# Zero-padded operands on TensorE in a two-layer diffusion backbone on one core

## The chip, the core and the metric

The kernel runs on one core of one Trainium2 chip. The core has a matrix engine (TensorE, PE in the profile, with its weight loads shown apart as PEld), three engines for elementwise work (VectorE is DVE, ScalarE is ACT, GpSimd is POOL) and a queue processor for transfers (SyncE is SP). The metric is the device time of one execution in microseconds (us); lower is better. A difference under 0.3% (8 us here) can't be told from no change for this kernel.

## The reference

One inference step of a backbone with two layers and a width of 2048, for 512 latent tokens and 128 prompt tokens (640 columns in all). Each layer normalizes its input, multiplies it by one input projection of 7168 columns, gives the result to three groups of heads, and multiplies their outputs by one output projection.

```python
h = rmsnorm(x, norm_g) * (1 + scale) + shift
proj = jnp.matmul(h, w_in)                      # 2048 x 7168
q, k, v, ag, lx, lg, hv, hx1, hx0, hg = jnp.split(proj, SPLITS, axis=-1)
# differential attention: 8 heads, two components of 64 features each
s = jnp.einsum('bqhcd,bkhcd->bchqk', qblk, k) * scale
p = jax.nn.softmax(s, axis=-1)
w = p[:, 0] - lam * p[:, 1]
att = jnp.einsum('bhqk,bkhe->bqhe', w, v)
# hyena: a filter network gives two long filters, used through a spectrum
filt = jnp.matmul(hdn, w3).reshape(L, 2, HY_W) * decay      # hdn has 64 features
y = irfft(rfft(u, n=2 * L) * rfft(g, n=2 * L), n=2 * L)[:, :L]
...
return x + gate * jnp.matmul(concat([att, lru, hy]), w_out)
```

A latent query of the attention sees 256 cached keys and 512 latent keys (768); a prompt query sees the 128 prompt keys.

## The kernel before

Features lie on the 128 partitions and tokens on the columns. All matrix products are made at float32 accuracy from operands in two parts, `hi` (rounded to the engine's reduced float32) and `lo` (the rest): a product is hi x hi + hi x lo + lo x hi, three matmuls into the same accumulator (`mm3`, L715; `mms`, L707).

**The main product.** `gemm` (L401) makes 128 output features of a projection: 4 pieces of 4 chunks of the contraction; for each chunk 6 matmuls of 320 columns (L419, tile `g`). The weights of a piece come by a DMA (`wr`), ACT rounds them (`wh`, L177) and DVE makes the rest (`wl`, L178); there are four buffers of each. Between the pieces stand steps of `ada_steps` (L321), which computes the modulation of later phases on DVE (`adas`, L334).

**Attention.** `attention` (L1034) runs for 8 heads in each layer: projections of the queries, keys and values, rotation of queries and keys (`rope_rot`, L1023, on DVE, with scratch tiles `rs` and `rt`), the split of the queries of each component c into `qq` (64 rows of hi above 64 rows of lo, for c = 1 the other way round), and of the keys into `kk` (hi twice, on all 128 rows) and `kl` (lo, one tile, each component on its own 64 rows). `softmax_diff` (L1140) works on a block of 128 queries: for each component, two halves of 384 keys, and for each half two matmuls into PSUM tile `pS`: `kk` on 128 rows (hi x hi and lo x hi at once), and `kl` on 64 rows (`qq[c][cs]`, `kl[cs]`). These four are called a score group here; the prompt's has one half of 128 keys, so two matmuls. DVE then takes the row maximum out of `pS` (L1157), ACT the exponential with its sum `Z` (L1158), DVE the two normalizations and the difference (L1161 to L1164); the weights are turned by six transposes (L1100), split (`wth`, `wtl`) and multiplied by the values (18 matmuls). There is one buffer of `pS`. A head ends with the squares of its output: a product on POOL into `oq` (L1119), a square on ACT and a difference on POOL (L1121).

**Hyena.** `filters` (L571) makes the spectra of the filters: `filt` multiplies the 64 rows of the hidden layer `hid` by `w3` (L607; positions 0 to 383 on the lower partitions, the others on the upper ones), and `spec` multiplies by the tables of a Fourier transform (`tb`); time 256 stands apart, as products with a single row (`eh` and `el` against one row of the table `rw`). `hyena_u` (L752) makes the signal, with `ue` for time 256 (two rows); `hyena_conv` (L802) makes its spectrum (products with `ue`, two rows), multiplies, and transforms back (products with `rh` and `rl`, one row each). The frequency 512 is a product with one column of weights, into one row of PSUM. `filter_hidden` (L544) computes `hid` of both layers at the start and keeps it on chip.

The order on each engine is set by a scheduler from the program's text and its priorities; an engine takes its instructions in that order. The steps of the hyena filters and of the long convolution stand between the pieces of `gemm` calls.

## Time and profile before

| what | value |
|---|---|
| time, median of 3 runs | 2831.08 us (2827.84 to 2836.65) |
| profiled execution, span from first to last instruction | 2832.2 us |
| granted TensorE clock, mean | 0.988 of full speed |
| PE busy | 2722.8 us, 96% of the span |
| PEld busy | 2496.4 us, 88% |
| DVE busy | 1937.1 us, 68% |
| ACT busy | 1074.7 us, 38% |
| POOL busy | 246.7 us, 9% |

The span is the profiled execution's own time as far as the profile has it; it lies 1.1 us above the median. A matmul's record reaches from its start to its end, and the next one starts long before that, since they are pipelined: what a matmul costs PE is the distance from its start to the next start, not its duration. A row of the timeline merges equal instructions that follow each other ("x4"), and shows the start of the first and the time to the end of the last. "64*128" is the part of the array that a matmul uses, rows by columns. The number of columns behind it ("64x384") is what it streams.

### The profile page before, as it was taken

The numbers are of one execution on the slowest core, as the hardware profiler recorded it, in microseconds if no ns is written. First come the engines' busy times: TensorE is split into PE (matmuls) and PEld (weight loads), VectorE is DVE, ScalarE is ACT, GpSimd is POOL, SyncE is SP. The second block draws the span as 40 slices with busy tenths as digits, with TensorE's granted clock in tenths as the row PEclk, the third lists the DMA queues.
The fourth block names the chain that finished last, engine by engine and source line by source line (L and its number), as shares of the span: only waits on it lengthen the run. The fifth ranks groups of instructions, "written<-read, shape, count | busy, mean of one in ns | idle before, by whom it ended". The sixth has DMA issues, their size and how long they took to land. (4 is left out here: it accounts for less than half of the span.)

```text
span 2832.2 us, 45809 instructions
## 1 busy us (share of the span) xinstructions
PE 2722.8 (96%) x17539; PEld 2496.4 (88%) x17539; DVE 1937.1 (68%) x3507; ACT 1074.7 (38%) x1970; POOL 246.7 (9%) x332
## 2 busy tenths in 40 slices
PE   5999989999999999999999999999999999999998
PEld 3689888889888888899988999888888899889998
DVE  3578996876877787787779467867776655555333
ACT  4234544444444212132234255444444432213223
POOL 1001210000000220200001022000000021020000
PEclk9999999999999999999999999999999999999999
DMA  8863442322323544476665323322222142335333
GB/s 257 269 211 113 119 147 64 95 81 70 95 79 100 165 131 144 151 239 204 194 182 156 94 81 92 112 73 90 80 66 59 56 147 77 96 122 175 95 90 122
DMA packets 439271, 353.54 MB, mean 125 GB/s; under 512 B 26710, under 2 KB 367326, under 8 KB 438796
## 3 DMA queue, kind: packets, MB, share of 16 engines
q1 hardware_dynamic: 428618, 336.39, 39.2%
q10 hardware_dynamic: 9298, 9.03, 1.0%
q0 software_dynamic: 1136, 5.19, 0.5%
q8 instruction: 138, 2.26, 0.3%
q14 instruction: 81, 0.66, 0.1%
HBM read 315.60 MB, written 34.93 MB: 124 GB/s over the span
## 5 line engine op out<-in xcount | busy, mean ns | idle before, releaser
L419 PE MATMUL g<-A,wh 128*128 128x320 f32 x8320 | 1622.8, 313 | 0.7 <-DVE A L178 0.7
L419 PEld LDWEIGHTS g<-A,wh 128*128 128x128 f32 x8320 | 1316.0, 189 | 24.8 <-issue 18.0
L419 PE MATMUL g<-A,wl 128*128 128x320 f32 x4160 | 968.1, 312 | 0.0
L177 ACT CAST wh<-wr 128x512 fp32r<-128x512 f32 (+1 forms) x592 | 361.9, 613 | 1049.3 <-PE g L419 802.4
L419 PEld LDWEIGHTS g<-A,wl 128*128 128x128 f32 x4160 | 700.8, 189 | 9.3 <-issue 7.8
L178 DVE TENSOR_TENSOR wl<-wr,wh 128x512 fp32r<-128x512 f32 (+1 forms) x592 | 435.2, 738 | 389.9 <-ACT wh L177 369.1
L334 DVE SCALAR_TENSOR_TENSOR adas<-wa,cs,adas 128x512 f32<-128x512 f32 x480 | 360.2, 777 | 56.5 <-DMA wa<-in_w_ada 55.0
L1158 ACT ACTIVATE e<-e,mx 128x768 f32<-128x768 f32 (+1 forms) x160 | 133.5, 834 | 71.7 <-DVE e L1157 71.0
L1157 DVE TENSOR_SCALAR_CACHE_REDUCE e<-pS 128x768 f32<-128x768 f32 (+1 forms) x160 | 131.3, 821 | 38.7 <-PE pS L709 37.0
L709 PE MATMUL pS<-kl,qq 64*128 64x384 f32 (+1 forms) x288 | 122.6, 426 | 0.0
L709 PE MATMUL pS<-kk,qq 128*128 128x384 f32 (+1 forms) x288 | 109.0, 379 | 2.9 <-DVE e L1157 2.7
L1119 POOL TENSOR_TENSOR oq<-ot 128x640 f32<-128x640 f32 x16 | 22.2, 1389 | 1007.8 <-ACT ot L1115 559.8
L520 PE MATMUL gp<-A,wh 128*128 128x320 f32 x512 | 101.4, 316 | 1.0 <-ACT wh L177 1.0
L396 PE MATMUL g<-A,wh 128*128 128x320 f32 (+2 forms) x384 | 92.8, 324 | 8.2 <-DVE A L491 5.7
L709 PEld LDWEIGHTS pS<-kl,qq 64*128 64x128 f32 x288 | 52.7, 183 | 54.3 <-issue 50.9
L178 DVE TENSOR_TENSOR wtl<-pt,wth 128x512 fp32r<-128x512 f32 (+1 forms) x144 | 70.5, 524 | 42.6 <-ACT wth L177 42.2
L520 PEld LDWEIGHTS gp<-A,wh 128*128 128x128 f32 x512 | 79.2, 188 | 22.5 <-issue 10.6
L177 ACT CAST wth<-pt 128x512 fp32r<-128x512 f32 (+1 forms) x144 | 59.8, 459 | 87.1 <-PE pt L1100 84.9
L709 PEld LDWEIGHTS pS<-kk,qq 128*128 128x128 f32 x288 | 54.1, 188 | 29.0 <-issue 23.7
L396 PEld LDWEIGHTS g<-A,wh 128*128 128x128 f32 x384 | 67.1, 194 | 13.6 <-DVE A L491 7.9
L1389 DVE SCALAR_TENSOR_TENSOR xf<-g,mod,xo 128x128 f32<-128x128 f32 (+3 forms) x96 | 38.4, 434 | 56.5 <-PE g L419 23.9
L312 PE MATMUL pa<-wada,csw 128*32 128x512 f32 (+1 forms) x320 | 51.6, 562 | 23.7 <-DMA wada<-in_w_ada 23.5
(353 smaller groups left out, 3187.6 us busy)
## 6 DMA issues: line engine op xcount, KB each, us to landing
wr<-in_w_in SPq DMA_DIRECT2D x440, 256.0 KB
wa<-in_w_ada SPq DMA_DIRECT2D x256, 256.0 KB
wada<-in_w_ada SPq DMA_DIRECT2D x64, 512.0 KB
wr<-in_w_out SPq DMA_DIRECT2D x128, 256.0 KB
mx<-md SPq DMA_DIRECT2D x28, 320.0 KB
md<-ot SPq DMA_DIRECT2D x16, 320.0 KB
gm<-md SPq DMA_DIRECT2D x16, 320.0 KB
R<-rd SPq DMA_DIRECT2D x16, 320.0 KB
```

The lines of the kernel that those rows point to most:

```text
L177: self.nc.scalar.copy(hi, src)
L178: self.nc.vector.tensor_tensor(lo, src, hi.bitcast(F32), op=ALU.subtract)
L312: nc.tensor.matmul(acc[32 * q:32 * q + 32, :], lhsT=self.csw[:, k, :], rhs=w[:, j, :], start=k < 4, stop=k >= 12, tile_position=(0, 32 * q))
L334: nc.vector.scalar_tensor_tensor(acc[:, s], w, c, acc[:, s], op0=ALU.mult, op1=ALU.add)
L396: nc.tensor.matmul(p[:, j, o:o + c1 - c0], lhsT=w[:, c, :], rhs=rhs[k][x][:, c0:c1], start=(a == 0 and c == 0 and n == 0), stop=(a == 3 an ...
L419: nc.tensor.matmul(p[:, j, :HT], lhsT=w[:, c, :], rhs=rhs[k][x][:, j * HT:(j + 1) * HT], start=(a == 0 and c == 0 and n == 0), stop=(a == ...
L520: nc.tensor.matmul(p[:, j, :HT], lhsT=w[:, c, :], rhs=rhs[k0 + c][x][:, j * HT:(j + 1) * HT], start=(c == 0 and t == 0), stop=(c == n - 1 ...
L709: self.nc.tensor.matmul(out, lhsT=a, rhs=b, start=(n == 0), stop=(n == len(pairs) - 1))
L1119: nc.gpsimd.tensor_tensor(sq, ot, ot, op=ALU.mult)
L1157: V.tensor_scalar(e[:, :nk].rearrange("p (a b) -> p a b", a=nhf), ps[:, :nhf, :hw], -1.0, None, op0=ALU.mult, op1=ALU.min, accum_out=mx)
L1158: nc.scalar.activation(e[:, :nk], e[:, :nk], AF.Exp, scale=-1.0, bias=mx, accum_out=Z[:, c:c + 1])
L1389: V.scalar_tensor_tensor(x[:, a:b], p, mod[:, 32 + m, s:s + 1], xo[:, a:b], op0=ALU.mult, op1=ALU.add)
```

## The change

The operands that used 64, 32 or fewer rows of the array, or one column, are put into tiles of 128 partitions whose other rows are zero, and the products run over all 128 rows and 128 columns.

- Scores: `kl` becomes two tiles, one for each component, allocated once in a layer; the 64 rows that belong to the other component are set to zero once (POOL, 64 x 896 each). To make room, the scratch tile `rt` of `rope_rot` goes away and its values go to the buffer of `oq`.
- Filter network: `w3` gets two copies, each with the other 64 rows zero, and the product runs over all of `hid`. `hid` is written to DRAM at the start, and read back when `filters` begins.
- Spectra of the filters: `eh` and `el` become rows 0 and 32 of one tile `er`; the table row in `rw` stands on partitions 0 and 32 of a 128-partition table that is zero elsewhere. Two matmuls become one.
- The long convolution: `ue` has its parts on rows 0 and 32, made after the transposition and no longer before it; `rh` and `rl` become rows 0 and 32 of `rr`, and again two matmuls become one.
- Frequency 512: 128 columns of weights in the place of one; only row 0 of the result is read.

```diff
-    rowt = np.zeros((2, TCE_W + 256), f4)
-    rowt[:, 0:257] = tab(np.cos, np.array([256]), fe, 512)
...
+    rowt = np.zeros((128, TCE_W + 256), f4)
+    for p0 in (0, 32):
+        rowt[p0, 0:257] = tab(np.cos, np.array([256]), fe, 512)[0]
...
-            hid = self.tl(self.cst, [128, 384], s="hid") if b else self.tl(pool, [128, 384], tag="h1", bufs=2)
+            hid = self.tl(pool, [128, 384], tag="h1", bufs=2)
...
-        return hid
+        q.dma_start(self.hd[l], hid)
...
-        hid = self.hid[l]
+        hid = self.tl(pool, [128, 384], tag="hid")
+        q.dma_start(hid, self.hd[l])
...
-        w3 = self.tl(pool, [128, 2, 512], tag="w3")
-        for u in (0, 64):
-            q.dma_start(w3[u:u + 64], i["hy_w3"][l].rearrange("k (d c) -> k d c", d=2))
+        w3 = self.tl(pool, [128, 2, 2, 512], tag="w3")
+        for n, u in enumerate((0, 64)):
+            G.memset(w3[64 - u:128 - u, n], 0.0)
+            q.dma_start(w3[u:u + 64, n], i["hy_w3"][l].rearrange("k (d c) -> k d c", d=2))
+        er = self.tl(pool, [128, 256], F32R, tag="er")
+        G.memset(er.bitcast(F32), 0.0)
...
-                nc.tensor.matmul(ps[:, d * 256:(d + 1) * 256], lhsT=hid[us, t0:t0 + 128], rhs=w3[us, d, hs], start=True, stop=True,
-                                 tile_position=(us.start, 0))
+                nc.tensor.matmul(ps[:, d * 256:(d + 1) * 256], lhsT=hid[:, t0:t0 + 128], rhs=w3[:, u, d, hs], start=True, stop=True)
...
-                v["eh"], v["el"] = (self.tl(pool, [1, 256], F32R, tag=t) for t in ("eh", "el"))
-                self.split_v(v["eh"], v["el"], PM[0:1, 2, s, :])
+                self.split_v(er[0:1, :], er[32:33, :], PM[0:1, 2, s, :])
...
-                     extra=[(rw[0:1, self.roff(fc):self.roff(fc) + 128], x) for x in rows])
+                     extra=[(rw[:, self.roff(fc):self.roff(fc) + 128], x) for x in rows])
...
-                mm = [(tb[:, 0, r, off:off + 1], x[:, r, :]) for r in range(2) for x in (sh, sl)]
-                mm += [(rw[0:1, 256:257], x) for x in rows]
-                self.mms(ps[0:1, :256], mm)
+                mm = [(tb[:, 0, r, off:off + 128], x[:, r, :]) for r in range(2) for x in (sh, sl)]
+                mm += [(rw[:, 256:384], x) for x in rows]
+                self.mms(ps[:, :256], mm)
...
-        ue = self.tl(pool, [128, 2], F32R, tag="ue")
-        V.tensor_copy(ue[:, 0:1], u[:, 256:257])
-        V.tensor_tensor(ue[:, 1:2], u[:, 256:257], ue[:, 0:1].bitcast(F32), op=ALU.subtract)
...
-        nc.tensor.transpose(pt[:2, 0:128], ue.bitcast(F32), self.ident)
+        nc.tensor.transpose(pt[:, 0:128], u[:, 256:384], self.ident)
...
-        V.tensor_copy(st["ue", hf][:, cs], pt[:2, 0:128])
+        ue = st["ue", hf]
+        self.split_v(ue[0:1, cs], ue[32:33, cs], pt[0:1, 0:128])
...
-                             extra=[] if sd else [(rw[0:2, self.roff(fc):self.roff(fc) + 128], ue)])
+                             extra=[] if sd else [(rw[:, self.roff(fc):self.roff(fc) + 128], ue)])
...
-        rh = self.tl(hp, [1, 2, 256], F32R, tag="rh")
-        rl = self.tl(hp, [1, 2, 256], F32R, tag="rl")
-        self.split_v(rh, rl, y)
+        rr = self.tl(hp, [128, 2, 256], F32R, tag="rr")
+        nc.gpsimd.memset(rr.bitcast(F32), 0.0)
+        self.split_v(rr[0:1], rr[32:33], y)
...
-                self.mm3(ps[:, odd, :256 if odd else TCE_W], pairs, extra=[(x[:, odd, cs], rw[0:1, ro]) for x in (rh, rl)])
+                self.mm3(ps[:, odd, :256 if odd else TCE_W], pairs, extra=[(rr[:, odd, cs], rw[:, ro])])
...
-        t1 = self.tl(pool, [128, NL], tag="rt")
+        t1 = self.tl(pool, [128, T], tag="oq")[:, :NL]
...
-        kl = self.tl(pool, [128, NK], F32R, tag="kl")
...
-            self.split(kk[c][u], kl[u], ks[u])
+            self.split(kk[c][u], kl[c][u], ks[u])
...
-                self.mms(ps[:, hf, :hw], [(qq[c][:, q0:q0 + 128], kk[c][:, s]), (qq[c][cs, q0:q0 + 128], kl[cs, s])])
+                self.mms(ps[:, hf, :hw], [(qq[c][:, q0:q0 + 128], kk[c][:, s]), (qq[c][:, q0:q0 + 128], kl[c][:, s])])
...
+                kl = [self.tl(pool, [128, PAST + T], F32R, tag=f"kl{c}") for c in range(2)]
+                for c in range(2):
+                    nc.gpsimd.memset(kl[c][64 - 64 * c:128 - 64 * c].bitcast(F32), 0.0)
```

On PE, the third score group of the fourth head of layer 0 (`g` is the projection of the next head, `pS` the scores) stood before as

```order
L419 MATMUL g_1270_6564<-A_388,wl_6568 128x320 x2
L709 MATMUL pS_6373<-kk_1181_6168,qq_1159_6017 128x384
L709 MATMUL pS_6373<-kl_6170,qq_1159_6017 128x384
L709 MATMUL pS_6373<-kk_1181_6168,qq_1159_6017 128x384
L709 MATMUL pS_6373<-kl_6170,qq_1159_6017 128x384
L419 MATMUL g_1270_6564<-A_606,wh_6567 128x320 x2
L419 MATMUL g_1270_6564<-A_607,wh_6567 128x320 x2
```

and the changed program has there

```order
L420 MATMUL g_1266_6568<-A_390,wl_6572 128x320 x2
L713 MATMUL pS_6377<-kk_1178_6173,qq_1156_6022 128x384
L713 MATMUL pS_6377<-kl_747_3819,qq_1156_6022 128x384
L713 MATMUL pS_6377<-kk_1178_6173,qq_1156_6022 128x384
L713 MATMUL pS_6377<-kl_747_3819,qq_1156_6022 128x384
L420 MATMUL g_1266_6568<-A_608,wh_6571 128x320 x2
L420 MATMUL g_1266_6568<-A_609,wh_6571 128x320 x2
```

Nothing moved: the same four matmuls stand between the same neighbours, and the second of each pair now reads all rows of a tile `kl` of its component.

On PE, the end of a step of the filter spectra (`sh` and `sl` are the signal's parts, `pt` the result, then the next piece of `g`) stood before as

```order
L709 MATMUL pt_10135<-sl_10092,tb_9797 128x256
L709 MATMUL pt_10135<-sh_10091,tb_9797 128x256
L709 MATMUL pt_10135<-eh_10084,rw_9799 128x256
L709 MATMUL pt_10135<-el_10085,rw_9799 128x256
L419 MATMUL g_1898_9993<-A_1737,wh_10127 128x320 x2
L419 MATMUL g_1898_9993<-A_1738,wh_10127 128x320 x2
```

and now as

```order
L713 MATMUL pt_10139<-sl_10096,tb_9797 128x256
L713 MATMUL pt_10139<-sh_10095,tb_9797 128x256
L713 MATMUL pt_10139<-er_9825,rw_9799 128x256
L420 MATMUL g_1892_9999<-A_1741,wh_10131 128x320 x2
L420 MATMUL g_1892_9999<-A_1742,wh_10131 128x320 x2
```

The two matmuls with the single rows are one, and the rest stands as it did.

On DVE, the end of the third head of layer 0, where the rotation of the next head's queries begins (`rs` the shuffled queries, `rt` the first product, `qs` the result), stood before as

```order
L1028 STREAM_SHUFFLE rs_6011<-qs_6009 128x512
L1164 SCALAR_TENSOR_TENSOR e_1116_5789<-e_1119_5798,rz_5801,e_1116_5789 128x768
L1029 TENSOR_TENSOR rt_6012<-qs_6009,rope_3813 128x512
L178 TENSOR_TENSOR wl_6181<-wr_6178,wh_6180 128x512
L1157 TENSOR_SCALAR e_1130_5850,mx_5849<-pS_5846 128x128
L178 TENSOR_TENSOR wtl_5745<-pt_5806,wth_5744 128x4x128
L178 TENSOR_TENSOR wtl_5745<-pt_5813,wth_5744 128x2x128
L1161 RECIPROCAL rz_5853<-Z_5838 128x2
L1030 TENSOR_TENSOR rs_6011<-rs_6011,rope_3813 128x512
L1162 TENSOR_SCALAR rz_5853<-rz_5853,nlam_2123 128x1
L1163 TENSOR_SCALAR e_1127_5843<-e_1127_5843,rz_5853 128x128
L1031 TENSOR_TENSOR qs_6009<-rt_6012,rs_6011 128x512
```

and in the changed program, where the first product goes to `oq`, the rotation ends some rows later:

```order
L179 TENSOR_TENSOR wtl_5866<-pt_5863,wth_5865 128x128
L335 SCALAR_TENSOR_TENSOR adas_5534<-wa_7298,cs_122,adas_5534 128x512
L179 TENSOR_TENSOR wl_6215<-wr_6212,wh_6214 128x512
L179 TENSOR_TENSOR vl_6313<-vf_5883,vh_6312 128x256
L335 SCALAR_TENSOR_TENSOR adas_5534<-wa_7298,cs_122,adas_5534 128x512
L1033 TENSOR_TENSOR oq_6017<-qs_6014,rope_3817 128x512
L335 SCALAR_TENSOR_TENSOR adas_5534<-wa_7362,cs_122,adas_5534 128x512
L1035 TENSOR_TENSOR qs_6014<-oq_6017,rs_6016 128x512
L179 TENSOR_TENSOR wl_6249<-wr_6246,wh_6248 128x512
L335 SCALAR_TENSOR_TENSOR adas_5534<-wa_7362,cs_122,adas_5534 128x512
L179 TENSOR_TENSOR qq_1156_6022<-qs_6014,qq_1156_6022 64x640
```

The first product has moved behind the split of the values (`vl`) and the steps of `adas`, since POOL still reads `oq` of the head that ends; the two splits of the rotated queries into `qq` have moved with it.

## Rows read from the trace of the kernel before

**Rows 1.** The page's busy times: us, share of the span, instructions.
```profile
PE 2722.8 (96%) x17539; PEld 2496.4 (88%) x17539; DVE 1937.1 (68%) x3507; ACT 1074.7 (38%) x1970; POOL 246.7 (9%) x332
```

**Rows 2.** PE timeline, a score group: start us, us, what, how many.
```profile
611.39 0.75 PE L419 MATMUL g<-A,wh 128*128 128x320 f32 x4
...
612.27 0.34 PE L709 MATMUL pS<-kk,qq 128*128 128x384 f32 x1
612.54 0.44 PE L709 MATMUL pS<-kl,qq 64*128 64x384 f32 x1
...
613.65 0.70 PE L419 MATMUL g<-A,wh 128*128 128x320 f32 x3
```

**Rows 3.** PE timeline, full-array matmuls of 384 columns, end of the program.
```profile
2788.95 0.52 PE L396 MATMUL g<-A,wh 128*128 128x384 f32 x2
```

**Rows 4.** PE timeline, the prompt's score group.
```profile
640.25 0.22 PE L709 MATMUL pS<-kk,qq 128*128 128x128 f32 x1
...
640.66 0.56 PE L419 MATMUL g<-A,wl 128*128 128x320 f32 x2
```

**Rows 5.** PE timeline, end of a step of the filter spectra.
```profile
1002.66 0.28 PE L709 MATMUL pt<-sl,tb 128*128 128x256 f32 x1
1002.78 0.28 PE L709 MATMUL pt<-sh,tb 128*128 128x256 f32 x1
...
1003.42 0.86 PE L419 MATMUL g<-A,wh 128*128 128x320 f32 x4
```

**Rows 6.** Groups by form, whole run: count, busy us, mean ns, idle before.
```profile
L709 PE MATMUL pS<-kl,qq 64*128 64x384 f32 x256 | 112.2, 438 | 0.0
...
L607 PE MATMUL pt<-w,hid 64*128 64x256 f32 x80 | 22.6, 408 | 0.0
```

**Rows 7.** Tile view of rw: duration ns min/median/max, first and last start.
```profile
L709 PE MATMUL pt<-eh,rw x20: 270/381/383, 975.8 to 2442.3; 1*128 1x256 f32 x16, 1*1 1x256 f32 x4
...
L709 PE MATMUL pt<-ue,rw x20: 272/380/383, 1117.4 to 2525.2; 2*128 2x256 f32 x16, 2*1 2x256 f32 x4
...
L709 PE MATMUL pS<-rw,rh x16: 378/382/383, 1154.9 to 2544.8; 1*128 1x258 f32 x8, 1*128 1x256 f32 x8
```

**Rows 8.** Softmax stages: window, length; busy PE, PEld, DVE, ACT, POOL; clock.
```profile
612.25:641.80 29.55, 29.55 (x161) 22.95 (x159) 21.52 (x47) 15.75 (x34) 0.00 (x0) 1.00 0.13 37
547.75:583.80 36.05, 36.05 (x205) 29.43 (x204) 30.51 (x64) 17.45 (x37) 0.00 (x0) 1.00 0.33 96
...
676.80:719.00 42.20, 42.20 (x247) 35.61 (x246) 33.89 (x63) 22.86 (x43) 0.00 (x0) 1.00 0.20 57
```

**Rows 9.** DVE's groups in the first of these stages, idle time and its enders.
```profile
L1157 DVE TENSOR_SCALAR_CACHE_REDUCE e<-pS 128x768 f32<-128x768 f32 (+1 forms) x9 | 7.9, 883 | 3.2 <-PE pS L709 3.2
...
L178 DVE TENSOR_TENSOR wtl<-pt,wth 128x512 fp32r<-128x512 f32 (+1 forms) x6 | 3.1, 554 | 1.0 <-ACT wth L177 1.0
L178 DVE TENSOR_TENSOR wl<-wr,wh 128x512 fp32r<-128x512 f32 x4 | 2.8, 690 | 3.7 <-ACT wh L177 2.8 <-PE g L419 0.8
...
L1161 DVE RECIPROCAL rz<-Z 128x2 f32<-128x2 f32 x4 | 0.7, 166 | 1.8 <-ACT e L1158 1.8
```

**Rows 10.** DVE's groups in the second of them.
```profile
L1157 DVE TENSOR_SCALAR_CACHE_REDUCE e<-pS 128x768 f32<-128x768 f32 (+1 forms) x9 | 7.9, 880 | 1.1 <-PE pS L709 1.1
...
L178 DVE TENSOR_TENSOR wl<-wr,wh 128x512 fp32r<-128x512 f32 x5 | 3.4, 689 | 3.0 <-ACT wh L177 3.0
```

**Rows 11.** Busy time by engine in the hyena stages of both layers.
```profile
900.00:1230.00 330.00, 315.48 (x2042) 291.89 (x2042) 252.78 (x428) 77.47 (x149) 57.22 (x87) 0.98 0.49 152
...
2275.00:2600.00 325.00, 312.48 (x2054) 292.07 (x2054) 185.48 (x307) 82.24 (x151) 50.71 (x87) 0.99 0.41 125
```

**Rows 12.** What PE waited for, whole run: us, times, longest.
```profile
PE pt L774 <- DVE ue L770: 12.6, 8, 3.3
```

**Rows 13.** PE timeline at the low clock, after 3.26 us without work.
```profile
1029.79 1.11 PE L774 MATMUL pt<-ident,uS 128*128 128x128 f32 x4 [3.26 <-DVE ue L770]
...
1031.39 1.27 PE L419 MATMUL g<-A,wh 128*128 128x320 f32 x4
```

More of the change, by code (lines that the diff above doesn't have):

```diff
@@ L96, in shape_constants @@
     c["dft"] = split_const(full)
-    rowt = np.zeros((2, TCE_W + 256), f4)
-    rowt[:, 0:257] = tab(np.cos, np.array([256]), fe, 512)
-    rowt[:, TCE_W:] = tab(np.sin, np.array([256]), fo, 512)
+    rowt = np.zeros((128, TCE_W + 256), f4)
+    for p0 in (0, 32):
+        rowt[p0, 0:257] = tab(np.cos, np.array([256]), fe, 512)[0]
+        rowt[p0, TCE_W:] = tab(np.sin, np.array([256]), fo, 512)[0]
     c["dftrow"] = rowt
@@ L633, in spec @@
             sh, sl = v["sh", sd], v["sl", sd]
-            rows = () if sd else (v["eh"], v["el"])
+            rows = () if sd else (er,)
             ps = psT()
@@ L729, in load_tabs @@
         nc.gpsimd.dma_start(tb, i["dft"])
-        rw = self.tl(pool, [2, TCE_W + 256], F32R, tag="rw")
+        rw = self.tl(pool, [128, TCE_W + 256], F32R, tag="rw")
         nc.gpsimd.dma_start(rw, i["dftrow"])
@@ L777, in hyena_u @@
         if jj == 0:
-            for t, shape in (("uh", [128, 4, 256]), ("ul", [128, 4, 256]), ("ue", [2, 256])):
+            for t, shape in (("uh", [128, 4, 256]), ("ul", [128, 4, 256]), ("ue", [128, 256])):
                 st[t, hf] = self.tl(hp, shape, F32R, tag=f"{t}_{hf}")
+            nc.gpsimd.memset(st["ue", hf].bitcast(F32), 0.0)
         if j == 0:
@@ L833, in hyena_conv @@
             off = (256, TCE_W + 256)[s]
-            mm = [(tb[:, 0, r, off:off + 1], x[:, s * 2 + r, :]) for r in range(2) for x in (uh, ul)]
+            mm = [(tb[:, 0, r, off:off + 128], x[:, s * 2 + r, :]) for r in range(2) for x in (uh, ul)]
             if s == 0:
-                mm += [(rw[0:2, 256:257], ue)]
-            self.mms(ps[0:1, s * 256:(s + 1) * 256], mm)
+                mm += [(rw[:, 256:384], ue)]
+            self.mms(ps[:, s * 256:(s + 1) * 256], mm)
         y = self.tl(pool, [1, 2, 256], tag="yy", bufs=3)
@@ L1031, in rope_rot, with attention @@
         V.tensor_tensor(x, t1, sh, op=ALU.add)
-    def attention(self, l, hs, h, pool, before):
+    def attention(self, l, hs, h, kl, pool, before):
         nc, V = self.nc, self.nc.vector
@@ L1204, in run @@
         self.g1 = [dt([2, 3, 256], f"g1{l}") for l in range(DEPTH)]
+        self.hd = [dt([128, 384], f"hd{l}") for l in range(DEPTH)]
         self.rd = [dt([NH, T], f"rd{l}") for l in range(DEPTH)]
@@ L1271, in run @@
                     with self.pool("hid", 1, "right") as hp:
-                        self.hid = [self.filter_hidden(l, hp, lambda: self.psT("t")) for l in range(DEPTH)]
+                        [self.filter_hidden(l, hp, lambda: self.psT("t")) for l in range(DEPTH)]
             st2.close()
@@ L1313, in layer @@
                 fin = lambda: None
+                kl = [self.tl(pool, [128, PAST + T], F32R, tag=f"kl{c}") for c in range(2)]
+                for c in range(2):
+                    nc.gpsimd.memset(kl[c][64 - 64 * c:128 - 64 * c].bitcast(F32), 0.0)
                 for h in range(NH):
-                    fin = self.attention(l, hs, h, pool, fin)
+                    fin = self.attention(l, hs, h, kl, pool, fin)
                 fin()
```

5 lines of the change are left out of this document (2 added, 3 removed).

## The prediction

> **What bounds the kernel now.** I read the page's busy times first: PE is busy for 96% of the span, DVE for 68% [rows 1]. So the time is PE's queue of matmuls, and the question is what a matmul costs that queue. Its record doesn't say that; the distance from its start to the next start does. From 611.39 to the start of the score group at 612.27 PE starts six full-array matmuls of 320 columns (the four of the row, and the two with `wl` that stand behind them in the order of the section on the change): 0.88 / 6 = 0.147 us each [rows 2]. For 384 columns, two records end after 0.52 us where a single one takes 0.34, so 0.18 each [rows 2, 3]. For 256 columns it is 0.12 (1002.66 to 1002.78) [rows 5].
>
> Against that I read the products which the change touches. A score group of the fourth head lasts from 612.27 to 613.65, 1.38 us for four matmuls of 384 columns, where 4 x 0.18 = 0.72 would do; and the three `g` matmuls behind it take 0.70 where four take 0.75 (three would take 0.60), so about 0.10 of the change back is paid there [rows 2]. The prompt's group of two takes 0.41 (640.25 to 640.66) and 0.10 behind it (0.56 for two) [rows 4]. In a step of the filter spectra the last full matmul `sh` starts at 1002.78, and `g` behind the two one-row matmuls at 1003.42, 0.64 us for three of 256 columns, and `g` then takes 0.86 where four usually take 0.75 [rows 2, 5]. In every place the loss is the same: about 0.2 us on the way into a product with fewer rows and 0.2 on the way out, whether it has 64 rows or one. I call 0.39 the price of one visit.
>
> The Trainium skill ("TensorEngine Tiling (Array Packing)", Key Properties) says that changing the tiling mode drains TensorE; the trace agrees, with that 0.39 us for each visit.
>
> **What the change gives PE.**
> - Scores of 768 keys: 1.38 + 0.10 - 0.72 = 0.76 us a group. There are 256 `kl` matmuls of 384 columns, two in a group [rows 6], so 128 groups: 97 us.
> - Scores of the prompt: the trace has no pair of full-array 128-column matmuls of this kind. They can't be slower than the 256-column ones, 0.12, nor cost less than nothing, so the gain is 0.51 - 0.24 = 0.27 at least and 0.51 at most. I take 0.27, since 0.12 is the nearest row; 8 heads x 2 layers x 2 components make 32 groups: 9 us.
> - Filter spectra: 0.64 + 0.11 - 2 x 0.12 (the last `sh` and one `er`) = 0.51, 16 times (x16 with 128 columns) [rows 5, 7]: 8 us.
> - Products with `ue`: a visit of one matmul, 16 x 0.39 = 6 us. The way back with `rh` and `rl`: 16 pairs, priced as the filter spectra, 16 x 0.51 = 8 us [rows 7].
> - Filter network: 80 records of 256 columns in visits of four [rows 6], 20 x 0.39 = 8 us. Their own pace inside a visit I leave as it is.
> - Frequency 512: 4 visits each for `eh` and `ue` [rows 7], at most 0.39, so 0 to 3 us; I take 2. One column or 128 columns of weights: no charge, as weight loads run beside matmuls (PEld 88% busy under PE's 96%) [rows 1].
>
> That is 106 us in attention and 32 in the hyena stages, 138 us of PE's queue.
>
> **What DVE lets through.** In the softmax stage of a head the next score group needs the only `pS` buffer, which DVE's L1157 frees, and DVE takes its rows in order. So the stage can't become shorter than DVE's own work plus those of its waits that don't come from PE. A faster PE shortens waits that end with PE, or with the weights `wh`, which ACT makes once PE has let go of a buffer. It doesn't shorten waits for an exponential or for a cast of turned weights, which follow DVE's own work.
> - Eight of the 16 heads have a stage as the first window: 29.55 us, DVE busy 21.5 [rows 8]. Of the 8.0 us that DVE idles, 3.2 end with PE's scores and 3.7 with `wh` or PE; 1.8 with the exponential, 1.0 with `wth`, the small rest with others [rows 9]. PE alone would give 8 x 0.76 + 2 x 0.27 = 6.6 us; DVE's floor is 21.5 + 3.1 = 24.6, which gives 29.55 - 24.6 = 4.9. The larger floor decides: 4.9 x 8 = 39 us.
> - Two heads (the fifth of each layer) have 68 `g` matmuls in the middle of the stage, and DVE idles 8.3 of 42.2 us [rows 8]: PE's 6.6 comes through, 13 us.
> - The other six look as the second window, with steps of `adas` in between: DVE busy 30.5 of 36.05 [rows 8], waits for PE's scores 1.1 and for `wh` 3.0 [rows 10]. That gives 4.1 each, 25 us.
>
> Attention returns 77 of its 106 us. In the hyena stages DVE is busy for 253 of 330 us in layer 0 and 185 of 325 in layer 1 [rows 11], so it isn't the floor, but PE already has some 14 us of waits in each, on chains that start with PE's own results and shift with it. Of 16 us in each layer I let 12 and 15 through: 27 us.
>
> **Smaller edits.** PE waits 12.6 us, 8 times, in front of the transposes of `hyena_u`, last for the two one-column operations that made `ue` [rows 12]; both go. Between 0 and 12.6 us; by the nearest short operation on DVE (L1161, 0.166 each [rows 9]) 8 x 2 x 0.15 = 2 us, which I take. `ue` then gets two short rows behind the transposes, where nobody stands in line for it at once.
> The zeroing (two tiles of 64 x 896 and one of each of the others) lies on POOL, 9% busy [rows 1], well ahead of its use: nothing. If one of them were late, the first head or the first step would wait about a microsecond, once in a layer. The round trip of `hid` adds a POOL transfer behind POOL's early loads, and a load on ACT's queue beside that of `w3`, for which the same step waits: nothing, or a transfer of a few us once in a layer. The table `rw` grows from 2 to 128 partitions: likewise.
> The scratch of `rope_rot` in `oq` is the one new wait. DVE's first product of the next head's queries now waits for POOL's second operation of the head that ends; behind it stand steps of `adas` and the weights `wl` of `g`. The new order puts it behind the split of the values, some ten rows later than before, so the wait falls where the last head is done, and the four buffers of weights carry PE over a microsecond or two. The queries themselves are needed only after the projections of keys and values, 90 and more `g` matmuls (90 x 0.147 = 13 us) later: nothing.
>
> Sum: 77 + 27 + 2 = 106 us. The profiled span is 2832.2 and the median of the runs 1.1 below, so 2832 - 106 - 1 = 2725 us.
>
> **Rivals.**
> - *All of it comes back.* DVE gives way, because waits for the exponential shrink too once the score groups come earlier. For it: DVE is busy for only three quarters of the first window. Against it: those waits follow DVE's own rows. It gives 138 + 2 us: 2831 - 140 = 2691.
> - *DVE gives way less.* The waits for `wh` are only filling: when they go, others take their place, and only the waits for scores come back (3.2 us in eight heads, 1.1 in the rest), with half of the hyena gain: 8 x 3.2 + 8 x 1.1 + 16 = 50 us: 2781. For it: the second window, where DVE has 85%. Against it: `wh` follows PE at once in both windows.
> - *Nothing changes.* The loss isn't that of the rows but of the operands. Against it: it is the same with 64, two and one rows, in five different products. For it: nothing in the rows. 2831.
> The Trainium skill ("TensorE: Matmul & The Clock Gate", Why this matters for your kernels) has a rule which speaks for that rival: a single matmul with 32 rows takes as long as one with 128, and only running several at once pays. By it the padding would be worth nothing; the 1.38 us against 0.72 of a score group speak against it, since here such products alternate with full ones.
> - *Slower.* In the attention stages PE, which had next to no waits, gets short ones between score groups, and the granted clock falls to 1.2 GHz. Place and price: behind 3.26 us without work four `g` matmuls took 1.27 us and not 0.75 [rows 2, 13], some 0.8 us more for each us of work. It would eat the gain of 106 us when 106 / 0.8 = 130 us of the two attention stages (some 1000 us) ran so, and beyond that the kernel is slower, say 2860. Against it: by the chain above no new wait comes near 3 us.
>
> **How the numbers follow.** Forecast as above 0.75; all back 0.10; DVE gives way less 0.10; nothing 0.02; slower 0.03. The likeliest alone gives 2725, within 2700 to 2755 (the share of attention that DVE lets through between 55 and 100 us, the hyena stages between 17 and 32). The range reaches to the first two rivals and takes about half of each: 2688 to 2778. Under 0.3% (8 us) no change can be told. Faster 0.95, the same 0.02, slower 0.03.
>
> **What would show it.** Right: score groups of 0.7 us from first to last start and no longer row behind them; `er`, `ue` and `rr` at 0.12; DVE over 85% busy in a window such as the first, its waits for `wh` and for scores mostly gone, and PE idle in short pieces before `pS`, waiting for L1157, some 30 us in all; stages of 25 us for the first kind of head. Wrong: no PE waits in attention and stages of 23 us (all back); stages of 28 us (DVE earlier); score groups still over 1 us (nothing); stretches at the low clock inside the attention stages (slower); a wait of DVE for `oq` that reaches PE.

## The result and the profile after

The changed kernel takes 2728.68 us (median; 2720.85 to 2730.49), against 2831.25 before: a ratio of 0.963 with an interval of 0.962 to 0.965, or 102.6 us less. The forecast was 106 us less, 2725 us. The profiled execution's span is 2728.5 us, 103.7 less than that of the kernel before. The total came out within 4 us; the parts it is made of did not all do so.

The page's busy times, which answer to [rows 1]:

```profile
PE 2599.8 (95%) x17503; PEld 2485.5 (91%) x17503; DVE 1920.0 (70%) x3499; ACT 1076.9 (39%) x1970; POOL 261.6 (10%) x352
```

PE has lost 123 us of busy time and is still what bounds the kernel. The same score group as in [rows 2], in PE's timeline (start us, us, what, how many):

```profile
602.63 0.34 PE L713 MATMUL pS<-kk,qq 128*128 128x384 f32 x1
602.80 0.34 PE L713 MATMUL pS<-kl,qq 128*128 128x384 f32 x1
602.98 0.34 PE L713 MATMUL pS<-kk,qq 128*128 128x384 f32 x1
603.16 0.34 PE L713 MATMUL pS<-kl,qq 128*128 128x384 f32 x1
603.33 0.60 PE L420 MATMUL g<-A,wh 128*128 128x320 f32 x3
```

The group takes 0.70 us (602.63 to 603.33) where it took 1.38, each start 0.17 or 0.18 behind the last, and the three `g` matmuls behind it take 0.60 and no longer 0.70. The end of a step of the filter spectra, which answers to [rows 5], is as plain: `er` starts 0.12 after `sh`, and `g` 0.12 after `er`.

```profile
955.63 0.28 PE L713 MATMUL pt<-sh,tb 128*128 128x256 f32 x1
955.75 0.28 PE L713 MATMUL pt<-er,rw 128*128 128x256 f32 x1
955.87 0.31 PE L420 MATMUL g<-A,wh 128*128 128x320 f32 x1
```

So PE's own saving is what the prediction says. Where it went is best seen by taking matmuls that both programs have, paired by their place in PE's queue with the edited products left out, and subtracting their starts:

| stretch, by starts before | shift over the stretch, us | forecast |
|---|---|---|
| start to 410.20 (to 415.82 after) | +5.6 | 0 |
| attention of layer 0, to 935.49 (896.34) | -44.8 | -38 |
| hyena stage of layer 0, to 1225.82 (1172.53) | -14.1 | -13 |
| the 20 to 30 us behind it, to 1248.36 (1202.88) | +7.8 | 0 |
| to 1771.87 (1724.80) | -1.6 | 0 |
| attention of layer 1, to 2274.56 (2184.93) | -42.6 | -39 |
| hyena stage of layer 1, to 2557.86 (2451.78) | -16.5 | -16 |
| to 2818.60 (2715.10) | +2.6 | 0 |

Attention returned 87 us and not 77, the hyena stages 31 and not 29; and 16 us were lost in places where nothing was forecast. PE's longest waits that bear on this (engine, line, what it waited for: us, times, longest):

```profile
PE pt L775 <- DVE uS L771: 11.8, 8, 2.3
PE pt L1064 <- ACT ks L1060: 7.5, 5, 2.3
PE pa L313 <- DMA wada<-in_w_ada: 7.4, 5, 3.3
...
PE g L420 <- ACT A L178: 5.0, 1, 5.0
...
PE pS L713 <- DVE e L1159: 3.4, 5, 2.0
...
PE pS L1198 <- DMA xt<-in_x_prompt: 2.7, 1, 2.7
```

The first stands where [rows 12] stood with 12.6 us. The second was 1.9 us in one place before. The waits for `A` and for `xt` of the prompt, which both stand right behind layer 0's hyena stage here, were 0.3 and 0.5 us there. The one before `pS` was 2.7 us in two places.

### The profile page after: what moved, and what is told of

It reads as the page before. It is cut to its first block, busy times and chain, and to the rows that moved or that the text cites. A ratio compares the mean times of both kernels' runs of the same rounds, so it can differ in the third digit from the quotient of the medians.

```text
span 2728.5 us, 45802 instructions
## 1 busy us (share of the span) xinstructions
PE 2599.8 (95%) x17503; PEld 2485.5 (91%) x17503; DVE 1920.0 (70%) x3499; ACT 1076.9 (39%) x1970; POOL 261.6 (10%) x352
## 5 line engine op out<-in xcount | busy, mean ns | idle before, releaser
L179 DVE TENSOR_TENSOR wl<-wr,wh 128x512 fp32r<-128x512 f32 (+1 forms) x592 | 429.2, 728 | 339.0 <-ACT wh L178 323.9
L713 PE MATMUL pS<-kk,qq 128*128 128x384 f32 (+1 forms) x288 | 100.3, 348 | 3.9 <-DVE e L1159 3.4
L713 PE MATMUL pS<-kl,qq 128*128 128x384 f32 (+1 forms) x288 | 95.2, 331 | 0.0
L1166 DVE SCALAR_TENSOR_TENSOR e<-e,rz,e 128x768 f32<-128x768 f32 (+1 forms) x80 | 70.6, 882 | 1.7
```

The costliest lines, as they stand in the source:

```text
L179: self.nc.vector.tensor_tensor(lo, src, hi.bitcast(F32), op=ALU.subtract)
L713: self.nc.tensor.matmul(out, lhsT=a, rhs=b, start=(n == 0), stop=(n == len(pairs) - 1))
L1166: V.scalar_tensor_tensor(es[0][:, :nk], es[1][:, :nk], rz[:, 1:2], es[0][:, :nk], op0=ALU.mult, op1=ALU.add)
```

## Experiments

**The price of a visit.** Only the order inside a score group is changed, in the kernel before; no operand is padded:

```diff
-                self.mms(ps[:, hf, :hw], [(qq[c][:, q0:q0 + 128], kk[c][:, s]), (qq[c][cs, q0:q0 + 128], kl[cs, s])])
+                nc.tensor.matmul(ps[:, hf, :hw], lhsT=qq[c][:, q0:q0 + 128], rhs=kk[c][:, s], start=True, stop=False)
+            for hf in range(nhf):
+                s = slice(k0 + hf * hw, k0 + (hf + 1) * hw)
+                nc.tensor.matmul(ps[:, hf, :hw], lhsT=qq[c][cs, q0:q0 + 128], rhs=kl[cs, s], start=False, stop=True)
```

> The kernel before, with nothing padded, but a score group in another order: kk, kk, kl, kl in the place of kk, kl, kk, kl. All four matmuls, their rows and their results stay. Theory of the visits (a change between 64 and 128 rows costs 0.39 us there and back, whatever lies between): one visit less in each of 128 groups, 128 x 0.37 = 47 us of PE, most of which attention lets through: 2785 to 2795 us; a group takes 1.38 - 0.37 = 1.0 us from start to start. Rival, a matmul with 64 rows is slow by itself (0.34 us more each): no change, 2831, a group takes 1.38.

Measured: 2782.3 us (2780.3 to 2790.5), ratio 0.983 (0.980 to 0.986): 49 us less than before, with the same matmuls on the same 64 rows. The group of [rows 2] in its timeline:

```profile
601.48 0.51 PE L1154 MATMUL pS<-kk,qq 128*128 128x384 f32 x2
601.93 0.61 PE L1157 MATMUL pS<-kl,qq 64*128 64x384 f32 x2
602.47 0.71 PE L419 MATMUL g<-A,wh 128*128 128x320 f32 x3
```

0.99 us from start to start (601.48 to 602.47), 1.38 before: one visit less, 0.39 us less. That the slowness is the matmul's own falls. Start to start, such a group goes 0.18, 0.27, 0.28, 0.26 (means over the run, kk to kk first), and the `g` behind it pays 0.10 more: a change costs about 0.2 us, half of it one matmul later, and the second `kl` adds nothing to the 0.39 of a visit. It is the change of rows that costs. The Trainium skill ("TensorEngine Tiling (Array Packing)", Key Properties) says that a change of mode drains the engine; the runs agree in that the change has a price, 0.39 us there and back, which is paid by the change and not by the matmul. That a drain is what costs it, no run here shows.

**Scores alone, and all but the scores.** The first is the kernel before with this part of the diff (and the round trip of `hid`, for room):

```diff
-            self.split(kk[c][u], kl[u], ks[u])
+            self.split(kk[c][u], kl[c][u], ks[u])
...
-                self.mms(ps[:, hf, :hw], [(qq[c][:, q0:q0 + 128], kk[c][:, s]), (qq[c][cs, q0:q0 + 128], kl[cs, s])])
+                self.mms(ps[:, hf, :hw], [(qq[c][:, q0:q0 + 128], kk[c][:, s]), (qq[c][:, q0:q0 + 128], kl[c][:, s])])
...
-        t1 = self.tl(pool, [128, NL], tag="rt")
+        t1 = self.tl(pool, [128, T], tag="oq")[:, :NL]
```

> The kernel before with the padded scores alone (two kl tiles a layer, the scratch of the rotation in oq, and, for room, the round trip of hid); the hyena products keep their few rows. Theory of the visits: the two attention stages shorten as in the changed kernel, where aligning the matmuls of both traces gives 45 us in layer 0 and 43 in layer 1; so 2831 - 88 = 2743 us (2735 to 2752). Rival, most of the gain comes from the other edits (w3, er, ue, rr): 2780 or more. A stall of some 5 us at the start (a wait for wada), if the round trip of hid is its cause, shows here too; if it is chance, it may be missing.

The second is the changed kernel with these lines turned back.

> The changed kernel with the scores as before (one kl tile a head, 64 rows, the scratch of the rotation in a tile of its own); all other products padded. Theory: the hyena stages shorten by 16 us each inside, as in the changed kernel's trace. If the loss of 10 us at the end of layer 0's hyena stage (PE waits for the operand A and for xt) belongs to these edits, since PE's queue there has become shorter and the transfers have not, 2831 - 21 = 2810 us (2802 to 2816) and the loss is in this trace. If it is chance or comes from attention, 2831 - 32 = 2799.

Measured: scores alone 2745.8 us (2736.8 to 2753.4), ratio 0.969; all the rest 2812.1 us (2804.5 to 2818.2), ratio 0.993 (0.990 to 0.995). The two gains, 3.1% and 0.7%, make 3.8%, beside 3.7% for both together: no sign that they get in each other's way. The attention stages of the first, from the first score matmul to the last, take 447.4 and 443.7 us, those of the changed kernel 446.5 and 443.3, those of the kernel before 491.3 and 485.4. In the second, the wait for `A` (5.1 us) and that for `xt` (1.4) are there as in the changed kernel; in the first `A` is 2.2 and `xt` 0.3. So most of that loss comes with the hyena edits. The stall of some 5 us at the start (3.26 us for `wada`, then 1.2 GHz) is not in the first. So the round trip of `hid` alone does not bring it. Among kernels whose program is the same up to there it is in the profile of the one with `FS` at 4 (2.3 us) and missing in that of the rotation in place, both below, so it comes and goes with the execution; yet of the traces in which the modulation's products stand as in the kernel before, none of the four without the padded hyena operands has it, and six of the seven with them do (0.8 to 3.3 us). Whether these edits bring it about is open.

**One column.** The changed kernel, with this turned back for both products of frequency 512:

```diff
-                mm = [(tb[:, 0, r, off:off + 128], x[:, r, :]) for r in range(2) for x in (sh, sl)]
+                mm = [(tb[:, 0, r, off:off + 1], x[:, r, :]) for r in range(2) for x in (sh, sl)]
...
-                self.mms(ps[:, :256], mm)
+                self.mms(ps[0:1, :256], mm)
```

> The changed kernel, with the products for frequency 512 back to one column of weights and one row of the result (all 128 rows of the contraction stay). The prediction charged nothing for a column: no change, 2728 us (2720 to 2737), and start to start distances of 0.12 us in and out of these 16 products. Rival, few columns cost a visit as few rows do: 16 x 0.39 = 6 us more in these places, 2735.

Measured: 2721.6 us (2720.2 to 2728.6), ratio 0.961 (0.959 to 0.964), which overlaps that of the changed kernel. Start to start, a one-column matmul behind another takes 0.116 us, and one in front of a full `g` 0.116 (medians of 60 and 7). A single column costs nothing here, so this part of the change brought nothing.

**Does DVE set the length of the softmax stage?** L1166, the difference of the two softmaxes, is left out, in the changed kernel and (as L1164) in the one before:

```diff
-        V.scalar_tensor_tensor(es[0][:, :nk], es[1][:, :nk], rz[:, 1:2], es[0][:, :nk], op0=ALU.mult, op1=ALU.add)
```

> The changed kernel without L1166, the difference of the two softmaxes on DVE (the weights are then those of the first component alone): 1.02 us of DVE less in each of 64 blocks of 128 queries, 4.3 us less in a head's softmax stage, of the 19.5 to 30 that DVE is busy there. Theory that DVE holds back what attention doesn't return (53 us of visits gone in layer 0, 45 returned): the 8 us in layer 0 and 10 in layer 1 come back, the stage of the second head goes from 22.6 to about 22.0 us and that of the third (DVE 98% busy) by more: 2728 - 15 = 2713 us (2708 to 2720). If DVE sets the stage's length outright: 16 x 4.3 = 69 us less, 2660. If PE alone sets it: 2728.

> The kernel before without the same operation, L1164. PE waits for scores 2.7 us in the whole run, so DVE has room in every stage: no change, 2831 us (2823 to 2833). Were DVE the bound already before: up to 16 x 4.3 = 69 us less.

Measured: 2718.4 us (2715.8 to 2725.6) for the changed kernel so lightened, 10 less; 2828.4 for the lightened kernel before (ratio 1.000, 0.999 to 1.001). In its whole run the operation costs DVE 70.6 us; the two attention stages became 442.9 and 439.2 us long, 3.6 and 4.1 shorter. So DVE did not set their length as a whole. What came back is visible in PE's waits in the attention stage of layer 0. The changed kernel (420 to 875 us):

```profile
PE pt L1064 <- ACT ks L1060: 3.3, 3, 1.2
PE pS L713 <- DVE e L1159: 1.1, 3, 0.5
...
```

and the lightened one (420 to 870 us):

```profile
PE pS L713 <- DVE e L1159: 3.2, 3, 2.3
```

The wait for `ks` is gone there, and one for the buffer of scores has grown. The wait for `ks`, then, is one that DVE causes by being late.

**The rotation's scratch.** In the changed kernel ACT has, ahead of that wait (timeline):

```profile
586.50 1.48 ACT L178 CAST qq<-qs 64x640 fp32r<-64x640 f32 x2 [2.65 <-DVE qs L1035]
588.00 0.62 ACT L178 CAST wh<-wr 128x512 fp32r<-128x512 f32 x1
588.53 0.68 ACT L1060 COPY ks<-g 128x640 f32<-128x640 f32 x1
```

The split of the queries waits for the rotation on DVE, and the copy of the keys stands behind it on ACT's queue; PE's transposes of the keys wait for the copy. The rotation was moved behind other rows by the scratch in `oq`. The experiment takes the scratch away; the product is made in place:

```diff
-        t1 = self.tl(pool, [128, T], tag="oq")[:, :NL]
...
-        V.tensor_tensor(t1, x, self.rope[:, 0, :], op=ALU.mult)
+        V.tensor_tensor(x, x, self.rope[:, 0, :], op=ALU.mult)
...
-        V.tensor_tensor(x, t1, sh, op=ALU.add)
+        V.tensor_tensor(x, x, sh, op=ALU.add)
```

> The changed kernel, with the rotation of queries and keys worked in place, without any scratch for its first product (oq no longer waits for the square of the head that ends, and is no longer waited for). In the changed kernel PE waits for the copy of the keys (ks) in front of their transposes, 7.5 us in 5 places, and these transposes cost 9.0 us from the start of the matmul before them against 3.0 in the kernel before. Theory: the wait on oq makes the queries late on DVE, the split of the queries stands in front of the copy of the keys on ACT, and PE waits behind both; in place the old order returns, the cost falls from 9.0 to about 3.0: 2728 - 6 = 2722 us. Rival, the wait only shows that PE now arrives earlier, whatever the scratch: it stays, 2728.

Measured: 2718.3 us (2715.6 to 2722.7), ratio 0.960 (0.958 to 0.961). What the engines waited for in front of these transposes (weight loads and matmuls together: us, times), in the changed kernel and, second, with the rotation in place:

```profile
  ACT ks L1060: 18.0, 20
```

```profile
  ACT ks L1059: 6.5, 16
```

The kernel before has 6.5 in 16 places too. In starts of matmuls, the step from `g` to these transposes costs, beyond the 0.147 us of a `g`, 9.1 us in all in the changed kernel, 3.1 in this one and 3.1 before. The attention stages take 443.5 and 438.4 us, 3.0 and 4.9 less. The rest of the 10 us between the medians is not shown to be the scratch's: the stall at the start is missing in this profile.

**The end of layer 0's hyena stage.** PE's timeline of the changed kernel there:

```profile
1172.09 0.75 PE L420 MATMUL g<-A,wh 128*128 128x320 f32 x4
1172.68 0.45 PE L420 MATMUL g<-A,wl 128*128 128x320 f32 x2
1178.12 1.97 PE L420 MATMUL g<-A,wh 128*128 128x320 f32 x6 [4.99 <-ACT A L178]
```

The last store of the convolution is issued at 1170.38, the first load of `mx` behind it at 1172.18, and PE runs out at 1173.1; in the kernel before these were 1218.8, 1221.0 and 1226.9. The last store came 48.4 us earlier, the end of PE's queue some 54. Two ways to give it more cover. First, the steps of the convolution behind every piece of a gate's projection:

```diff
-GH, FS = 0, 3
+GH, FS = 0, 4
```

> The changed kernel, with the steps of the long convolution after each of the four pieces of a gate's projection, and not after three of them, so that the last of its 11 steps stands 4 pieces (4 x 24 matmuls x 0.147 = 14 us of PE) earlier. Theory: the loss of 10 us at the end of layer 0's hyena stage is a lack of cover: the loads of mx come behind the last store of the convolution, and PE's own queue runs out before they land. With 14 us more of cover the wait for A (5.0 us) and the one for xt (2.7 us) go, with the low clock behind each: 2728 - 10 = 2718 us, if the steps of the convolution, now closer together, don't wait more among themselves. Rival, the convolution's own chain of transfers sets the end: its steps wait in the earlier place for as long, 2728 or slower.

Measured: 2729.7 us (2726.2 to 2731.2), no change. PE's waits from 1090 to 1210 us:

```profile
PE pt L713 <- DVE y L802: 2.6, 2, 2.4
PE pt L713 <- ACT yh L178: 1.9, 2, 1.2
PE pS L1198 <- DMA xt<-in_x_prompt: 1.8, 1, 1.8
...
PE g L420 <- ACT A L178: 0.8, 1, 0.8
```

The wait for `A` fell from 5.0 to 0.8, and the convolution's steps, closer together, wait among themselves for as much. That is what the rival said; that the convolution's own chain of products, splits and transfers sets the end is argued from these waits.

Second, fewer steps of `adas` there, since DVE waits for their weights (4.5 us in this stretch) ahead of the products `gm`. The steps were moved ahead of attention, and in another kernel behind the stage:

```diff
-RATE = (dict(lru=1, att=.5, ag1=.75, hv=.75, ag2=1, out=1)
+RATE = (dict(lru=1.35, att=.5, ag1=.75, hv=.75, ag2=.5, out=1)
```

> The changed kernel, with half of the modulation's steps (adas) taken out of the stage of layer 0's long convolution and made in its first stage (lru) instead; the same 192 steps in all. In the changed kernel DVE waits there 4.5 us for the weights wa of adas, in order, ahead of the products gm that the last stores carry, and PE loses about 10 us at the end of the stage. Theory: these waits make the last stores late; with fewer of them the stores, the loads of mx and the operand A come earlier, and 5 to 8 us of the loss return: 2722 us. Rival, the end is set by the transfers of the convolution and of mx themselves (gm, md, mx, 14 x 320 KB): no change, 2728.

Measured: 2742.0 us (2735.8 to 2749.8), 13 slower. The wait for `A` did go down (1.2 us, and none for `xt`). But attention starts 4.9 us later than in the changed kernel (428.7 against 423.7), ends at the same time, and the last transpose of `xt` in the output projection comes 10.9 us later (1406.7 against 1395.8). A new wait of 6.6 us, for `sx` in the filters' stage, accounts for some of that; the rest was not traced, since the scheduler put PE's work there into another order. The form with `out=1.15` in place of the higher first rate was tried on the fastest variant (below):

> The faster variant (rotation in place, modulation of the first stage in larger groups) with half of the modulation's steps (adas) taken out of the stage of layer 0's long convolution, and made in the output projection behind it (its rate goes from 1 to 1.15 a piece), not ahead of attention, where the moved steps cost 12 us. Theory: the wait for A (5.1 us in that variant) and the low clock behind it mostly go, as they did when the steps were moved ahead, and the output projection, with DVE busy two thirds of its time, takes the steps for nothing: 2712 - 6 = 2706 us. Rival, the weights wa land late there too, as the loads of mx and xt already fill the transfers at its beginning (70% of the DMA engines' time): 2712 or slower.

Measured: 2719.1 us (2712.5 to 2724.9), ratio 0.960 (0.958 to 0.961), 7 above that variant's median. The wait for `A` is gone from its trace; but layer 1's attention starts 1.1 us later than in the variant (1722.1 against 1721.0), so what was won at the border was gone again by then. A new wait of PE in the output projection of layer 0, 4.9 us for `xf`, took some of it, and where the rest went was not traced. The two profiled executions took the same time (2712.5 and 2712.4 us), so the 7 us between the medians are in no trace. Moving the steps, in either direction, made nothing faster as a whole.

**Column tiles.** The modulation's products in the first stage use 32 columns of the array each, four side by side. In the changed kernel a full matmul of 320 columns ahead of them costs 0.238 us and not 0.147, and the last of them 0.523. The products were taken in larger groups:

```diff
-                    ada_to(done + (2 if kn == 4 or gi else 1))
+                    if n % 2:
+                        ada_to(done + (4 if kn == 4 or gi else 2))
```

> The changed kernel, with the modulation's products of the first stage (wada, 32 columns of the array each, four side by side) taken 8 at a time behind every second block of gp and not 4 behind each. Start to start, a full matmul in front of them costs 0.24 us and not 0.147, and the last of them 0.52 where 512 columns alone take 0.23, so a change of the columns seems to cost a visit too, 0.38 us. Theory that it does: half of some 40 visits go, 20 x 0.38 = 8 us less, 2720, unless the transfers of wada, which land one after the other, make PE wait longer for the second four. Rival, the 0.52 is the products' own time: 2728.

Measured: 2712.3 us (2706.9 to 2715.3), ratio 0.958 (0.956 to 0.960), so 16 us faster than the changed kernel, twice the forecast. But the 0.38 us that the expectation takes for a visit is too high: it compares 0.523 with the 0.23 of 512 columns on the whole array, and that isn't what four of these products cost each other. A visit of eight in the changed kernel, and one of sixteen here (PE's timeline):

```profile
75.78 1.07 PE L313 MATMUL pa<-wada,csw 128*32 128x512 f32 x8
76.78 0.86 PE L521 MATMUL gp<-A,wh 128*128 128x320 f32 x4
```

```profile
127.42 1.92 PE L313 MATMUL pa<-wada,csw 128*32 128x512 f32 x16
129.27 0.85 PE L521 MATMUL gp<-A,wh 128*128 128x320 f32 x4
```

Eight take 1.00 us from start to start, sixteen 1.85, so four more cost 0.43, and only 0.1 of the 0.523 is the way out. In this the rival was nearly right: most of it is the products' own time. With 0.09 us ahead of the visit and 0.1 in the row behind it (0.86 for four, 0.75 elsewhere) a visit costs about 0.3 us. The trace explains only some of the gain: the scheduler made 36 visits of 45, not half of them, 9 x 0.3 = 2.7 us; and the stall at the start, which the profile of the changed kernel has, is missing (4.7 us by the shift). Some 4 us more came little by little behind the first stage. That the visits made the whole gain is not shown.

Together with the rotation in place:

> The changed kernel with the rotation in place and with the modulation's products of the first stage in larger groups, as in the run with fewer visits of column tiles (2712). If the two gains are separate: 2712 - 6 = 2706 us. If the wait for the keys is not the scratch's, 2712.

Measured: 2711.9 us (2707.9 to 2712.5), ratio 0.957 (0.956 to 0.958). The attention stages are 2 us shorter each than with the larger groups alone, and the step to the transposes of the keys is down to 3.1 us, but the medians of the two can't be told apart. These two are the fastest kernels of the study, some 4.2 to 4.3% below the kernel before.

## Why the prediction was right, and where it was not

- *PE's saving, 138 us.* Right. A group went from 1.38 + 0.10 to 0.70, `er` costs 0.12, and the run with the other order showed that 0.39 is the price of a change of rows and back. By starts of matmuls, the score groups and the row behind each lost 52 us in either layer, 104 of the 106 reckoned for attention.
- *What DVE lets through, 77 us of 106.* The failed step, by 10 us to the low side. It took DVE's own work plus those of its waits that don't come from PE as a floor, 24.6 us of the 29.55 of [rows 8]. The stages in rows of the same cut, from the first score group to the last (window, length; busy PE, PEld, DVE, ACT, POOL; clock), before:

```profile
612.25:640.70 28.45, 28.45 (x154) 21.85 (x152) 20.45 (x45) 15.27 (x34) 0.00 (x0) 1.00 0.13 38
547.75:582.20 34.45, 34.45 (x195) 27.84 (x193) 28.91 (x62) 17.16 (x36) 0.00 (x0) 1.00 0.34 100
676.80:718.20 41.40, 41.40 (x243) 34.81 (x241) 33.09 (x62) 22.86 (x43) 0.00 (x0) 1.00 0.20 58
```

and after:

```profile
602.63:625.20 22.57, 22.55 (x154) 21.39 (x152) 19.54 (x45) 14.98 (x32) 0.00 (x0) 1.00 0.16 46
542.44:571.20 28.76, 28.25 (x195) 27.52 (x193) 28.13 (x60) 16.86 (x35) 0.00 (x0) 1.00 0.40 117
661.58:695.95 34.37, 33.92 (x231) 32.80 (x229) 29.80 (x57) 21.36 (x40) 0.00 (x0) 1.00 0.25 72
```

The first kind gave 5.9 us (forecast 4.9), the second 5.7 (4.1). The third gave 7.0 (6.6), but with 231 matmuls in it and not 243: 12 of `g`, 1.8 us, stand elsewhere in the new order, so like for like it gave 5.3. For all 16 heads that is an estimate of 8 x 5.9 + 6 x 5.7 + 2 x 5.3 = 92 us and not 77; the late keys, below, took some of it back. In the first PE works without a pause, 22.55 of 22.57 us: PE still sets it, and DVE, 87% busy, only touches. DVE's groups in that stage (busy, mean ns of one | idle before, and what ended it):

```profile
L1159 DVE TENSOR_SCALAR_CACHE_REDUCE e<-pS 128x768 f32<-128x768 f32 (+1 forms) x9 | 7.9, 881 | 0.6 <-ACT e L1160 0.2 <-PE pS L713 0.2 <-DVE e L1166 0.2
...
L179 DVE TENSOR_TENSOR wtl<-pt,wth 128x512 fp32r<-128x512 f32 (+1 forms) x6 | 3.0, 550 | 0.2 <-ACT wth L178 0.2
...
L179 DVE TENSOR_TENSOR wl<-wr,wh 128x512 fp32r<-128x512 f32 x3 | 2.1, 690 | 2.8 <-ACT wh L178 2.8
```

Against [rows 9]: the waits for PE's scores went (3.2 to 0.2), as forecast. The 2.8 us for `wh` stand in both lists, but most of that wait lies ahead of the stage: it ends at 612.83 before and at 603.19 after, 0.6 us inside either window. The prediction took it whole, so the waits that it names (3.2, 3.7, 1.8 and 1.0) come to more than the 8.0 us of idle time that they should fill; the floor does not use it. Of the waits that were to stay, that for `wth` went (1.0 to 0.2) and the exponential's fell (1.8 to 1.4): they end with another engine, but they too give way when the scores come earlier. And DVE's busy time isn't a fixed sum: the same 45 instructions, up to the end of the last, are busy for 20.48 us in the stage before and for 19.86 after, with the same durations (0.883 and 0.881 for the reading of the scores). Where they stand close, one starts before the record of the one ahead has ended, and a floor made of busy time is too high. The second kind is at DVE's edge, 28.13 of 28.76 us. Taking 70.6 us of DVE's work away gave 7.8 us in attention, so DVE was no floor for the stages as a whole. By the prediction's own signs, too, the outcome lies towards "All of it comes back": DVE is 87% busy in the first window and its waits for scores are gone, but the stage, cut as in [rows 8], takes 23.7 us and not 25, and PE idles before `pS` for 3.4 us and not for some 30.
- *The scratch in `oq`, priced at nothing.* Wrong by 6 us in the step to the transposes of the keys, and by 8 in the length of the attention stages, where the longest of these waits has some 3 us at the low clock behind it (below). The prediction followed the late rotation on DVE and to the first use of the queries by PE; it did not follow it on ACT, where the split of the queries stands in front of the copy of the keys. The wait was found on a third engine. With it, 87 of the 104 us came through; without it 95.
- *The hyena stages, 27 us, and 2 for the transposes.* Inside they gave 31 (14.1 and 16.5), nearly all of PE's 32, so PE's waits there, as forecast, shift with it. But the step ended at the stage's border: behind it PE now overtakes the chain of stores and loads that feeds the output projection, and lost 7.8 us in layer 0 and some 2 in layer 1. A transfer that had cover only because PE was slow was not among the prediction's costs.
- *The waits at the transposes of `hyena_u`.* 2 us forecast of 12.6; 0.8 came: with `ue` gone the transposes wait for `uS`, the operation that stood just before it on DVE (11.8 us).
- *The start.* 5.6 us were lost before attention, most of it by one wait for `wada`. The forecast has nothing for it; whether it is the spread of the runs or comes with the edits is open (above).
- *Rivals.* "Nothing changes" is refuted by the group's 0.70 us, and the rule that the prediction weighed for it (a single matmul with few rows is as fast as a full one) holds inside a visit, as the second `kl` of a pair shows, but not for the way in and out. "DVE gives way less" (2781) is far off. "All of it comes back" (2691) was 19 us too high in attention, the forecast 10 too low. "Slower" has its sign: two stretches of some 3 us at the low clock stand in layer 1's attention, behind waits of 2.3 and 2.0 us, so the argument that no new wait comes near 3 us did not keep them away. They are too few to matter as that rival would have it; the kernel before has two as well, and the clock's mean is 0.987 (0.988 before). Its price of 0.8 us is 0.7 by its own rows (0.52 over 0.75).

So the sum was right by two errors of about equal size: attention and the hyena stages gave 12 us more than forecast (10 and 2), and the start and the ends of the two hyena stages took 14 back, net. That the total came within 4 us is luck in this part.

## What to carry to other kernels

Where products with few rows stand singly between full ones, read the distance from start to start around them: each change of rows and back cost 0.39 us here, whatever the matmul did in between, so zero rows are cheap, and so is putting like beside like in the order. When a bounding engine gets faster, look at each border of its stages for a transfer that had cover only because of the lost time. Follow a step that is moved through the queue of every engine that uses its result, to what stands behind it there.

## What the hardware showed beyond that

- The price of a change differs with what is changed: 0.39 us there and back for 64 rows in a score group, about 0.3 for four tiles of 32 columns in the first stage (0.09 ahead, 0.1 on the way out, 0.1 in the row behind). A product with one column on all 128 rows costs no change (0.116 us from start to start).
- After a wait of 3.3 us at the start, of 5.0 and 2.7 us behind the hyena stage, and of 2.3 and 2.0 us in layer 1's attention, PE runs at 1.2 GHz for a while, so that a wait costs more than its length. In the timeline at the start, and in that attention stage:

```profile
95.36 1.58 PE L313 MATMUL pa<-wada,csw 128*32 128x512 f32 x4 [3.26 <-DMA wada<-in_w_ada]
96.87 1.43 PE L521 MATMUL gp<-A,wh 128*128 128x320 f32 x4
...
1782.25 0.47 PE L1064 MATMUL pt<-ident,ks 128*128 128x128 f32 x1 [2.29 <-ACT ks L1060]
```

Four `gp` matmuls take 1.43 us there, and 0.75 elsewhere; the wait of 3.3 us moved what follows by 4.7. The granted clock, the number ahead of the last two, in two such stretches:

```profile
96.87:98.23 1.36, 1.36 (x6) 1.03 (x4) 0.00 (x0) 0.00 (x0) 0.00 (x0) 0.50 0.48 105
1782.25:1785.25 3.00, 3.00 (x12) 3.00 (x13) 2.93 (x8) 0.00 (x0) 0.00 (x0) 0.50 0.79 239
```

The length of the wait alone doesn't tell it: in the kernel before such stretches follow waits of 1.31 and 1.40 us for `pS` (at 746.99 and 1983.00), and with the rotation in place the same wait for `pS` in layer 1 took 2.77 us (to 1909.99), with a granted clock of 1.00 behind it.
